# New latency estimates for the planner that orders the attention phases

## The chip, the cores and the metric

The kernel runs on one core of a Trainium2 chip. The metric is the device time of one launch in microseconds (us), the median of several runs. The core's engines are TensorE (PE) for matrix products, VectorE (DVE), ScalarE (ACT), GpSimd (POOL), and SyncE (SP), which issues the DMAs. Each runs its own list of instructions in order, and semaphores make one wait for another.

## The reference

Two consecutive layers of a trunk work on 256 tokens of width 1024, with 256 rows of memory. All is float32.

```python
for layer in range(2):
    x = x + 0.5 * swiglu(rms_norm(x), w_gate, w_up, w_down)
    h = rms_norm(x)
    if layer == 0:   # even: 4 differential heads beside 8 stick-breaking heads, one projection in, one out
        x = x + diff_stickbreak_mixer(h, ...)
    else:            # odd: latent attention, 16 heads, keys and values from a low-rank product, rotary part of 32
        x = x + mla_mixer(h, ...)
    x = x + memory_cross_attention(rms_norm(x), rms_norm(mem), ...)   # 4 heads of 128
    x = x + 0.5 * swiglu(rms_norm(x), w_gate, w_up, w_down)
```

In the latent attention, keys and queries are normalised by head over 96 columns (64 plain and 32 rotated), and the softmax is causal by chunks of 64. In the cross-attention the memory's keys and the queries are normalised by head, and all 256 memory rows are seen.

## The kernel before

The kernel keeps x on the chip and streams all weights. Each float32 product is computed as three matmuls of rounded halves, one each in L284, L285 and L286. So each weight tile that arrives (DMA, L247) is cast by ACT into its high half (L249), and DVE subtracts to get the low half (L251). There are two raw buffers and three slots of halves (`HL`), and a tile is asked for two items ahead of its use (`LOOK`). SP issues the transfers; one that reuses a raw buffer goes out when DVE has read the old tile.

PSUM is cut into banks by purpose: three for products ("mm"), two for scores ("s"), two for turns ("t") and one for attention outputs ("o"). A turn is a transposition by PE (L792), four blocks into one bank, from which ACT or DVE copies them.

The phases are: a feed-forward half, the even mixer (214 to 312 us of the span), the first cross-attention (to about 360), two feed-forward halves, the latent mixer (from about 725), the second cross-attention (to about 890), and a last feed-forward half. PE's order is the program's own. In the attention phases a planner writes it: `run()` (L437) holds several generators (tasks). Each yields what it needs next: banks, a weight, events (`after`), or a pause (`lat`). The planner keeps a clock of its own in which only PE's work costs time (`spend`), and takes the ready task with the lowest priority number. All else is a guess by number: `drop(ps, d)` says that a bank is free d us later, `signal(ev, d)` says that an event is there d us later, and the tables `EST_X0`, `EST_X1`, `EST_AB` and `EST_MLA` hold these d. Arrivals of weights are guessed by `weight_ready` with `WTIME`. These numbers set the order of PE alone, by the order in which the code emits its work; the framework's scheduler then orders ACT, DVE, POOL and SP around it when the program is built.

The names that matter below:

- Even mixer: `values(t)` (L1185) makes the differential heads' output (L1190), whose norm runs over ACT (L1194), DVE (L1196, L1197), POOL (the power, L467) and DVE (L1201). `turn_o` (L1207) turns it, and `out_g` (L653) multiplies it with the output weights in pieces of six matmuls. `mem_k` (L834) makes the memory's keys for the cross-attention; their norm ends in L852, and after `lat` they are turned.
- Cross-attention: `attend(hp)` (L910) for two pairs of heads: scores (L917), softmax (reduction L770, exponentials L779, scaling L784), two turns copied by DVE (L800) and ACT (L798), `out` (L936) and its split into halves (ACT L486, DVE L487). The event `src` releases the output pieces of that pair.
- Latent mixer: `keys(hf, t)` (ACT L1291 to L1294, DVE L1299, L1300, POOL L467, DVE L1313, POOL L1315), `turn_k(hf)` with four turns copied by ACT (L1330), `queries(n, t)` (ACT L1344, L1347; DVE L1352, L1357, L1358, L1362; POOL L1354 and L467), and `attend(n)` (L1427) for four groups of four heads: two turns copied by DVE (L1435), scores (mask L322, L1448), softmax, three turns, `out` (L1481) and its split.

The lines of the functions that the change touches are `yield dict(t=1, lat=7.0)` in `mem_k` and `drop(pt, 0.9)` in `turn_k`.

Of the kernel before, what the change touches and what calls it, by code (L numbers as in the profile page):

```python
# [49 lines left out]
RAW = 2  # L50
BANKS = {"mm": 3, "s": 2, "t": 2, "o": 1}
WTIME = 4.41
SLOTS_MLA = (29, 11)
AB_ORDER = ('ka', 'qa', 'vb', 'va', 'k0', 'k1', 'v0')
T_ORDER = (0, 1)
KRAW = True
PREADD = True

EST_X0 = {'scale': 3.59, 'rq': 1.14, 'psd': 1.46, 'sp': 2.8, 'p1': 4.06, 'p2': 0, 'o': 1.32, 'src': 8.83}
EST_X1 = {'scale': 2.31, 'rq': 1.14, 'psd': 1.46, 'sp': 2.8, 'p1': 3.39, 'p2': 0.0, 'o': 1.18, 'src': 8.83}  # L60
EST_AB = {'b': 1.33, 'va': 1.47, 'rot': 14.92, 'st1': 6.44, 'st2': 0.14, 'z': 1.55, 'sto': 2.4, 'src': 0.79, 'T': 0.74, 'sp': 3.0, 'pc': 8.7, 'pcT': 1.4, 'po': 4.35, 'oa': 8.7, 'srco': 1.25}
PRIO_MLA = [1, 2, 4.2, 3.9, 4.4, 2.3]
PRIO_AB = [1, 6.1, 4.1, 6.9, 6.9, 0.5]
EST_MLA = {'latd': 1.52, 'scale': 11.0, 'r': 1.8, 'kr': 4.06, 'pk': 2.4, 'pv': 1.23, 'v': 1.73, 'k': 6.43, 'kT': 0.9, 'q': 7.82, 'qT': 2.38, 'cs': 3.11, 'sp': 6.25, 'p1': 3.36, 'p2': 0.68, 'p3': 0.75, 'o': 0.58, 'src': 0.8}
MLA_ORDER = (('k', 0), ('kv', 0), ('kv', 1), ('q', 0), ('q', 1), ('k', 1), ('q', 2), ('q', 3), ('v', 0))
HL = 3

# [93 lines left out]
def trunk_kernel(ctx, tc, wflat, xT_d, xtok_d, memT_d, memtok_d, gains_d, rows_d, cst_d, out_d):  # L161
# [34 lines left out]
    def al():  # L196
        return alloc("f")
# [4 lines left out]
    def rel(*ts):  # L202
        for t in ts:
            key, t = ar["own"].pop(id(t))
            ar[key].append(t)

    def sm():
        return T("sm", [P, 16], 24)
# [10 lines left out]
    offs, o = [], 0  # L219
# [92 lines left out]
    def gcol(c):  # L312
        return gains[:, c:c + 1]
# [70 lines left out]
    class Event:  # L384
        t = None
# [8 lines left out]
    def take(tag):  # L394
        ps = ps_(tag)
        i = min(range(len(od.bank[tag])), key=lambda i: od.bank[tag][i])
        od.bank[tag][i] = INF
        od.own[id(ps)] = (tag, i, ps)
        return ps

    def drop(ps, dur):
        tag, i, _ = od.own.pop(id(ps))
        od.pend.append((lambda t, tag=tag, i=i: od.bank[tag].__setitem__(i, t), dur))

    def signal(ev, dur):
        od.pend.append((lambda t, ev=ev: setattr(ev, "t", t), dur))

    def spawn(prio, gen):
        t = Order()
        t.gen, t.prio, t.seq = gen, prio, len(od.all)  # L410
        od.all.append(t)
        t.req = next(gen)
        t.ready = od.now + od.cost + t.req.get("lat", 0.0)
        od.live.append(t)
# [50 lines left out]
    def rsqrt(v, n, dst=None):  # L465
        y = (dst or sm())[:, :n]
        G.tensor_tensor(out=y, in0=v, in1=mhalf[:, 0:n], op=ALU.pow)  # L467
        return y
# [162 lines left out]
    def tm_g(key, xg):  # L631
        yield dict(w=key, mm=1)
        w = weight(key, 256)
        ps = take("mm")
        for t in range(2):
            for k in range(KT):
                a = tuple(z[:, t * P:(t + 1) * P] for z in xg[k])
                mm3(ps[:, t * S:(t + 1) * S], a, (w[0][:, k, :], w[1][:, k, :]), k == 0, k == KT - 1)
                if k % 4 == 3 and (t, k) != (1, KT - 1):
                    yield {}  # L640
        done(key)
        return ps
# [145 lines left out]
    def transpose4(srcs, rows_=P):  # L788

        ps = take("t")  # L790
        for i, s in enumerate(srcs):
            PE.transpose(ps[0:rows_, i * P:(i + 1) * P], s, ident)  # L792
            spend(0.11)
        return ps
# [39 lines left out]
    def mem_k(l, c, events):  # L834

        ps = yield from tm_g((f"memk{l}", c), memstate["x"])
        rm = memstate["rs"]

        def norm():
            yield dict(after=events)  # L840
            k = al()
            for t in range(2):
                A.activation(k[:, t * S:(t + 1) * S], ps[:, t * S:(t + 1) * S], AF.Identity, scale=rm[:, t:t + 1])
            drop(ps, 1.2)
            sq = al()
            G.tensor_tensor(out=sq, in0=k, in1=k, op=ALU.mult)
            v = sm()[:, 0:4]
            V.tensor_reduce(out=v, in_=sq.rearrange("p (a b) -> p a b", b=P), axis=AX.X, op=ALU.add)
            V.tensor_scalar(out=v, in0=v, scalar1=1.0 / P, scalar2=EPS, op0=ALU.mult, op1=ALU.add)
            r = rsqrt(v, 4)  # L850
            k3 = k.rearrange("p (a b) -> p a b", b=P)
            V.tensor_tensor(out=k3, in0=k3, in1=r.unsqueeze(2).to_broadcast([P, 4, P]), op=ALU.mult)  # L852
            yield dict(t=1, lat=7.0)
            pt = transpose4([k3[:, t * 2 + j, :] for j in range(2) for t in range(2)])
            kt = al()
            A.activation(kt, pt, AF.Identity, scale=gcol(G_XK + l))
            drop(pt, 0.9)
            rel(k, sq)
            memstate["k", l, c] = kt

        spawn(1, norm())
# [15 lines left out]
    def cross(l, gc):  # L877
        EST_X = (EST_X0, EST_X1)[l]
        xg = st.xg
# [89 lines left out]
    def mixer_ab(gc):  # L969
# [12 lines left out]
        def products():  # L982
            for key in ("qb", "kb"):
                for c in range(2):
# [5 lines left out]
                    def evac_b(key=key, c=c, ps=ps):  # L990
# [7 lines left out]
                        drop(ps, 0.9)  # L998
                        signal(ev[key, c], EST_AB['b'])

                    spawn(0, after([ev["rb"]], evac_b))
            for key in AB_ORDER:
# [8 lines left out]
                for c in range(2):  # L1011
# [6 lines left out]
                    drop(ps, 1.2)  # L1018
                    signal(ev[key, c], EST_AB['va'])
                if dst is None:  # L1020
# [4 lines left out]
        def rotate(key):  # L1025
# [20 lines left out]
            if key == "qa":  # L1046
                rqs["r"] = r
            signal(ev[key], EST_AB['rot'])


        def strict(z):

            dg = z.rearrange("p (a b) -> p a b", b=S)[:, :, 0:P]
            G.affine_select(out=dg, in_=dg, pattern=[[0, 2], [1, P]], compare_op=ALU.is_gt, fill=0.0,
                            base=0, channel_multiplier=-1)
# [3 lines left out]
        def stick(hq, g):  # L1059
# [25 lines left out]
            for i, (z, (sp, hh, hl)) in enumerate(zip(zs, sps)):  # L1085
                yield dict(lat=EST_AB['st2'] if i else EST_AB['st1'])
                for h_ in (hh, hl):
# [5 lines left out]
                strict(w_)  # L1093
                drop(z, EST_AB['z'])
                ws.append(w_)
                rel(sp, hh, hl)
            yield dict(lat=EST_AB['sto'], o=1 - g, after=[ev["vb", hq]] + [ev["po", hq]] * g)
            if g == 0:
# [126 lines left out]
    def mixer_mla(gc):  # L1225
# [6 lines left out]
        lat = {"ckv": ([], []), "cq": ([], [])}  # L1232
        rl, kk, kf, vt, kT, qf, qv, rqs = {}, {}, {}, {}, {}, {}, {}, {}

        def latent(key, gc0, ps):
# [8 lines left out]
            sqs.append(sq)  # L1244
            drop(ps, EST_MLA['latd'])

        def scale(key, dim):
            yield dict(t=1, lat=EST_MLA['scale'], after=[ev["rs"]])
            sqs = lat[key][1]
            if PREADD:  # L1250
                if len(sqs) == 2:
                    G.tensor_tensor(out=sqs[0], in0=sqs[0], in1=sqs[1], op=ALU.add)
                G.tensor_tensor(out=sqs[0][:, 0:S], in0=sqs[0][:, 0:S], in1=sqs[0][:, S:2 * S], op=ALU.add)
                ps, cs = colsum([[sqs[0][:, t * P:(t + 1) * P]] for t in range(2)], take)
            else:
                ps, cs = colsum([[q[:, j * S + t * P:j * S + (t + 1) * P] for q in sqs for j in range(2)]
                                 for t in range(2)], take)
            rl[key] = latent_scale(cs, 2, dim, st.var)
            rel(*sqs)
            drop(ps, 0.8)  # L1260
            signal(ev["r" + key], EST_MLA['r'])

        def shared_key(krT):

            yield dict(t=1, lat=EST_MLA['kr'], after=[ev["rs"]])
            pt = take("t")
# [17 lines left out]
        def keys(hf, t, pk, pv):  # L1284
# [9 lines left out]
            A.activation(v, pv, AF.Identity, scale=rc[:, t:t + 1])  # L1294
            drop(pk, EST_MLA['pk'])
            drop(pv, EST_MLA['pv'])
            vt[hf].append(v)
# [24 lines left out]
        def turn_k(hf):  # L1322
            kT[hf] = []
            for g in range(4):
                yield dict(t=1, after=[ev["k", hf, t] for t in range(2)])
                a = g // 2
                pt = transpose4([kf[hf][t][a][:, ((2 * g + j) % 4) * 96:((2 * g + j) % 4 + 1) * 96]
                                 for j in range(2) for t in range(2)], 96)
                d = al()
                A.activation(d[0:96, :], pt[0:96, :], AF.Identity, scale=gqk[0:96, :])  # L1330
                kT[hf].append(d)
                drop(pt, 0.9)
                signal(ev["kT", hf, g], EST_MLA["kT"])
                if g % 2:
                    rel(*[kf[hf][t][a] for t in range(2)])
# [185 lines left out]
    with arena(*SLOTS_FFN):  # L1521
        ffn(0, 1, G_FFN + 16, True)
        ffn(1, 0, G_MIX + 8, False, 1)
    with arena(*SLOTS_MLA):
        mixer_mla(G_XM + 8)
# [78 lines left out]
```

## Time and profile before

| what | value |
|---|---|
| median of 3 runs | 1082.94 us (1082.51 to 1085.24) |
| the profiled execution | 1083.22 us |
| its span | 1081.5 us |
| granted TensorE clock | 0.998 of full speed |
| busy: PE / DVE / ACT / POOL | 98% / 72% / 61% / 11% |
| chain that ended last | PE 87%, DVE 5%, ACT 3%, issue 2%, DMA 2%, POOL 1% |
| PE L792 (turn) waits for DVE L852 | 4.1 us, 3 times |
| PE L792 waits for DVE L784 | 2.3 us, once |
| PE L1448 waits for DVE L1435 | 1.6 us, 2 times |
| PE L792 waits for POOL L1315 | 1.6 us, once |
| PE L936 waits for DVE L800 | 1.1 us, 2 times |
| PE L792 waits for ACT L1330 | 0.9 us, once |
| PE L322 waits for ACT L779 | 0.8 us, once |
| PE L1104 waits (issue) | 0.8 us, once |

The busy share tells how much of the span an engine worked; the chain that ended last is followed back from the last instruction, and tells on which engine the time lay. The waits give PE's idle time by the instruction that waited and the one that released it. A row of a timeline gives the start within the span, the duration, the engine, the line, what was written and read, and in brackets the idle time before it with its releaser. A row with x8 is eight instructions one after another.

### The profile page before, as it was taken

What the parts mean: (1) busy time and instruction counts of PE and PEld (TensorE: products, weight loads), DVE (VectorE), ACT (ScalarE), POOL (GpSimd) and SP (SyncE); (2) the same over time, 40 slices, a digit from 0 to 9 for tenths busy, and PEclk for the clock granted to TensorE, in tenths of its full rate; (3) what the DMA queues carried; (4) which work ended last, traced back from release to release, by engine and by line L of the source; (5) the groups of instructions that cost most, each with busy time, mean ns of one, the idle gap of its engine ahead of it and who ended that gap; (6) DMA issues with size and microseconds to landing.
All of it is one profiled execution on the core that took longest, in us unless ns stands there. A gap on an engine that the chain in (4) does not pass through costs nothing.

```text
span 1081.5 us, 23308 instructions
## 1 busy us (share of the span) xinstructions
PE 1059.9 (98%) x9034; PEld 1042.2 (96%) x9034; DVE 782.3 (72%) x1908; ACT 655.3 (61%) x1775; POOL 124.3 (11%) x160
## 2 busy tenths in 40 slices
PE   8999999999899999999999999999889999999998
PEld 8999999998899999999999999999878999999998
DVE  5988766677867877776777777665788778777653
ACT  6767565567755665555666655565866667555542
POOL 0200000134121200000100000002640212000000
PEclk9999999999999999999999999999999999999999
DMA  8776556625245355555556565554241544555561
GB/s 287 247 252 205 207 188 212 195 89 186 84 156 191 120 192 196 195 185 196 204 182 226 197 215 179 186 193 164 99 157 45 163 145 156 196 195 196 185 228 56
DMA packets 51232, 193.36 MB, mean 179 GB/s; under 512 B 5808, under 2 KB 8368, under 8 KB 36016
## 3 DMA queue, kind: packets, MB, share of 16 engines
q1 hardware_dynamic: 50976, 191.81, 52.1%
q8 instruction: 71, 1.16, 0.4%
q14 instruction: 41, 0.34, 0.1%
q10 hardware_dynamic: 144, 0.05, 0.0%
HBM read 190.79 MB, written 1.05 MB: 177 GB/s over the span
## 4 chain that ended last, share of the span: by engine, by line
PE 87%; DVE 5%; ACT 3%; issue 2%; DMA 2%; POOL 1%; SPq 0%; DVEq 0%; ACTq 0%; POOLq 0%
PE mm L284 27%; PE mm L285 27%; PE mm L286 27%; DMA wr<-wflat 2%; DVE wl L251 1%; ACT slotf L779 1%; PE t L792 1%; POOL sm L467 1%; DVE sm L770 1%; PE t L475 0%; PE s L1448 0%; PE s L917 0%; ACT wh L249 0%; POOL sl L467 0%; PE o L1481 0%
## 5 line engine op out<-in xcount | busy, mean ns | idle before, releaser
L249 ACT CAST wh<-wr 128x256 fp32r<-128x256 f32 (+1 forms) x1216 | 440.7, 434 | 289.5 <-PE mm L285 235.2
L251 DVE TENSOR_TENSOR wl<-wr,wh 128x256 fp32r<-128x256 f32 (+1 forms) x1216 | 500.7, 468 | 121.3 <-ACT wh L249 116.6
L284 PE MATMUL mm<-xh,wh 128*128 128x256 f32 x1552 | 429.7, 277 | 1.6 <-ACT wh L270 1.6
L286 PE MATMUL mm<-xh,wl 128*128 128x256 f32 x1552 | 427.8, 276 | 0.0
L285 PE MATMUL mm<-xl,wh 128*128 128x256 f32 x1552 | 427.7, 276 | 0.0
L284 PEld LDWEIGHTS mm<-xh,wh 128*128 128x128 f32 x1552 | 291.4, 188 | 2.4 <-ACT wh L270 2.1
L286 PEld LDWEIGHTS mm<-xh,wl 128*128 128x128 f32 x1552 | 291.4, 188 | 0.6 <-DVE wl L271 0.3
L285 PEld LDWEIGHTS mm<-xl,wh 128*128 128x128 f32 x1552 | 291.4, 188 | 0.4
L284 PE MATMUL mm<-slotr,wh 128*128 128x256 f32 x896 | 247.6, 276 | 0.3 <-ACT slotr L481 0.3
L285 PE MATMUL mm<-slotr,wh 128*128 128x256 f32 x896 | 246.7, 275 | 0.4 <-DVE slotr L482 0.4
L286 PE MATMUL mm<-slotr,wl 128*128 128x256 f32 x896 | 246.6, 275 | 0.0
L284 PEld LDWEIGHTS mm<-slotr,wh 128*128 128x128 f32 x896 | 168.2, 188 | 1.0 <-ACT slotr L481 0.6
L285 PEld LDWEIGHTS mm<-slotr,wh 128*128 128x128 f32 x896 | 168.2, 188 | 0.7 <-DVE slotr L482 0.6
L286 PEld LDWEIGHTS mm<-slotr,wl 128*128 128x128 f32 x896 | 168.2, 188 | 0.0
L530 POOL TENSOR_TENSOR acc<-acc,sq 128x256 f32<-128x256 f32 x49 | 39.2, 801 | 527.4 <-ACT sq L522 526.8
L738 DVE TENSOR_TENSOR slotf<-mm,rb 128x512 f32<-128x512 f32 x43 | 29.7, 691 | 51.6 <-PE mm L286 51.6
L481 ACT ACTIVATE xh<-x,gains 128x256 fp32r<-128x256 f32 x64 | 32.2, 507 | 28.9 <-DVE x L510 26.0
L779 ACT ACTIVATE slotf<-s,sm,sl 128x256 f32<-128x256 f32 (+1 forms) x64 | 32.8, 523 | 20.5 <-DVE sm L773 14.6
L728 DVE TENSOR_TENSOR slotf<-mm,rb 128x512 f32<-128x512 f32 x43 | 29.7, 690 | 20.9 <-PE mm L286 20.6
L510 DVE SCALAR_TENSOR_TENSOR x<-mm,x 128x256 f32<-128x256 f32 x64 | 26.9, 420 | 23.4 <-PE mm L286 23.4
L482 DVE SCALAR_TENSOR_TENSOR xl<-x,gains,xh 128x256 fp32r<-128x256 f32 x64 | 37.0, 582 | 4.2 <-ACT xh L481 4.0
L487 DVE TENSOR_TENSOR slotr<-slotf,slotr 128x512 fp32r<-128x512 f32 (+1 forms) x52 | 35.7, 690 | 3.4 <-ACT slotr L486 3.2
(203 smaller groups left out, 1150.4 us busy)
## 6 DMA issues: line engine op xcount, KB each, us to landing
wr<-wflat SPq DMA_DIRECT2D x118, 1024.0 KB, 4.8
wr<-wflat SPq DMA_DIRECT2D x179, 256.0 KB, 4.0
wr<-wflat SPq DMA_DIRECT2D x16, 768.0 KB, 4.3
slotf<-memT SPq DMA_DIRECT2D x8, 256.0 KB, 3.3
wr<-wflat SPq DMA_DIRECT2D x2, 512.0 KB, 8.0
slotf<-xtok SPq DMA_DIRECT2D x4, 256.0 KB, 7.0
slotf<-memtok SPq DMA_DIRECT2D x4, 256.0 KB, 4.0
out<-x SPq DMA_DIRECT2D x8, 128.0 KB, 2.0
```

The source lines that it names most:

```text
L249: A.copy(hi[:, a:b], raw[:, a:b])
L251: e.tensor_tensor(out=lo[:, a:b], in0=raw[:, a:b], in1=hi[:, a:b].bitcast(F32), op=ALU.subtract)
L284: PE.matmul(out, a[0], b[0], start=first, stop=False, **kw)
L285: PE.matmul(out, a[0], b[1], start=False, stop=False, **kw)
L286: PE.matmul(out, a[1], b[0], start=False, stop=last, **kw)
L481: return (A.activation(hi, src, AF.Identity, scale=g), V.scalar_tensor_tensor(out=lo, in0=src, scalar=g, in1=hi.bitcast(F32), op0=ALU.mult ...
L482: V.scalar_tensor_tensor(out=lo, in0=src, scalar=g, in1=hi.bitcast(F32), op0=ALU.mult, op1=ALU.subtract))
L487: V.tensor_tensor(out=lo, in0=src, in1=hi.bitcast(F32), op=ALU.subtract)
L530: G.tensor_tensor(out=st.acc, in0=st.acc, in1=sq, op=ALU.add)
L728: V.tensor_tensor(out=t.rearrange("p (a b) -> p a b", b=S), in0=pg.rearrange("p (a b) -> p a b", b=S), in1=rbb, op=ALU.mult)
L738: V.tensor_tensor(out=u.rearrange("p (a b) -> p a b", b=S), in0=pu.rearrange("p (a b) -> p a b", b=S), in1=rbb, op=ALU.mult)
L779: A.activation(p[:, i * w:(i + 1) * w], sps[:, i * w:(i + 1) * w], AF.Exp, bias=nb[:, i:i + 1], scale=r, accum_out=sums[:, i:i + 1])
```

## The change

Only numbers change. In both cross phases `o` rises to 1.6 and `src` falls from 8.83 to 2.0. In the even mixer `va`, `sp` and `srco` rise. In the latent mixer `k`, `kT`, `qT` and `p2` rise and `q` falls; one more buffer slot is given to that phase (`SLOTS_MLA`). The memory's keys wait 9.0 instead of 7.0 ahead of their turn, and the bank of a turned key is held 1.6 instead of 0.9 in the planner's account.

```diff
-SLOTS_MLA = (29, 11)
+SLOTS_MLA = (30, 11)
-EST_X0 = {'scale': 3.59, 'rq': 1.14, 'psd': 1.46, 'sp': 2.8, 'p1': 4.06, 'p2': 0, 'o': 1.32, 'src': 8.83}
-EST_X1 = {'scale': 2.31, 'rq': 1.14, 'psd': 1.46, 'sp': 2.8, 'p1': 3.39, 'p2': 0.0, 'o': 1.18, 'src': 8.83}
-EST_AB = {'b': 1.33, 'va': 1.47, 'rot': 14.92, 'st1': 6.44, 'st2': 0.14, 'z': 1.55, 'sto': 2.4, 'src': 0.79, 'T': 0.74, 'sp': 3.0, 'pc': 8.7, 'pcT': 1.4, 'po': 4.35, 'oa': 8.7, 'srco': 1.25}
+EST_X0 = {'scale': 3.59, 'rq': 1.14, 'psd': 1.46, 'sp': 2.8, 'p1': 4.06, 'p2': 0, 'o': 1.6, 'src': 2.0}
+EST_X1 = {'scale': 2.31, 'rq': 1.14, 'psd': 1.46, 'sp': 2.8, 'p1': 3.39, 'p2': 0.0, 'o': 1.6, 'src': 2.0}
+EST_AB = {'b': 1.33, 'va': 2.8, 'rot': 14.92, 'st1': 6.44, 'st2': 0.14, 'z': 1.55, 'sto': 2.4, 'src': 0.79, 'T': 0.74, 'sp': 4.4, 'pc': 8.7, 'pcT': 1.4, 'po': 4.35, 'oa': 8.7, 'srco': 2.2}
-EST_MLA = {'latd': 1.52, 'scale': 11.0, 'r': 1.8, 'kr': 4.06, 'pk': 2.4, 'pv': 1.23, 'v': 1.73, 'k': 6.43, 'kT': 0.9, 'q': 7.82, 'qT': 2.38, 'cs': 3.11, 'sp': 6.25, 'p1': 3.36, 'p2': 0.68, 'p3': 0.75, 'o': 0.58, 'src': 0.8}
+EST_MLA = {'latd': 1.52, 'scale': 11.0, 'r': 1.8, 'kr': 4.06, 'pk': 2.4, 'pv': 1.23, 'v': 1.73, 'k': 8.4, 'kT': 1.5, 'q': 7.0, 'qT': 2.9, 'cs': 3.11, 'sp': 6.25, 'p1': 3.36, 'p2': 1.2, 'p3': 0.75, 'o': 0.58, 'src': 0.8}
-            yield dict(t=1, lat=7.0)
+            yield dict(t=1, lat=9.0)
-                drop(pt, 0.9)
+                drop(pt, 1.6)

```

The instructions and SP's order are the same in both programs. Three places show what the planner makes of the numbers.

ACT in the latent mixer (L1344 and L1347 make a query tile, L1330 copies turned keys, L249 casts a weight). Before:

```order
L1344 ACTIVATE slotf_9740<-mm_10350,sl_10171 128x384
L1330 ACTIVATE slotf_9733<-t_10372,small 96x512
L1347 ACTIVATE slotf_9732<-slotf_9740 128x384
L1330 ACTIVATE slotf_9745<-t_10378,small 96x512
L1344 ACTIVATE slotf_9746<-mm_10384,sl_10171 128x384
L249 CAST wh_10419<-wr_10418 128x512
L1347 ACTIVATE slotf_9750<-slotf_9746 128x384
L1330 ACTIVATE slotf_9751<-t_10406,small 96x512
L1330 ACTIVATE slotf_9737<-t_10412,small 96x512
L249 CAST wh_10419<-wr_10418 128x512 x2
```

After:

```order
L1347 ACTIVATE slotf_9740<-slotf_9739 128x384
L1344 ACTIVATE slotf_9732<-mm_10373,sl_10172 128x384
L249 CAST wh_10408<-wr_10407 128x512
L1347 ACTIVATE slotf_9733<-slotf_9732 128x384
L1330 ACTIVATE slotf_9745<-t_10395,small 96x512
L1330 ACTIVATE slotf_9746<-t_10401,small 96x512
L249 CAST wh_10408<-wr_10407 128x512 x2
L1330 ACTIVATE slotf_9750<-t_10432,small 96x512
L1330 ACTIVATE slotf_9737<-t_10462,small 96x512
```

A cast (the row of L249 without x2) stood behind two L1330; now it stands ahead of them, and all four L1330 come after it.

DVE in the first cross-attention, from the last scaling of the probabilities on (L784; L487 is the low half of a head pair's output, L800 the copy of turned probabilities). Before:

```order
L784 TENSOR_SCALAR slotf_2666<-slotf_2666,sm_4655 128x256 x2
L487 TENSOR_TENSOR slotr_2682<-o_4663,slotr_2682 128x512
L800 COPY slotf_2658<-t_4684 128x512
L251 TENSOR_TENSOR wl_4705<-wr_4703,wh_4704 128x256 x7
L487 TENSOR_TENSOR slotr_2682<-o_4696,slotr_2682 128x512
```

After:

```order
L784 TENSOR_SCALAR slotf_2666<-slotf_2666,sm_4655 128x256 x2
L487 TENSOR_TENSOR slotr_2682<-o_4663,slotr_2682 128x512
L251 TENSOR_TENSOR wl_4686<-wr_4684,wh_4685 128x256 x8
L800 COPY slotf_2658<-t_4711 128x512
L487 TENSOR_TENSOR slotr_2682<-o_4737,slotr_2682 128x512
```

The copy L800 stood right behind the low half of pair 0; now eight weight subtractions stand between them.

ACT at the end of the even mixer (L1194 begins the norm behind the second `values`, L1176 copies turned probabilities, L843 and L871 copy the memory's keys and values, L856 copies its turned keys, L481 makes the high half of the turned output). Before:

```order
L249 CAST wh_3968<-wr_3967 128x512 x4
L1176 COPY slotf_2659<-t_3995 128x512
L856 ACTIVATE slotf_2665<-t_4001,gains 128x512
L1194 ACTIVATE slotf_2662<-o_4019 128x512
L871 ACTIVATE slotf_2672<-mm_3982,small 128x256
L871 ACTIVATE slotf_2679<-mm_3982,small 128x256
L856 ACTIVATE slotf_2669<-t_4061,gains 128x512
L249 CAST wh_4068<-wr_4067 128x512 x4
L481 ACTIVATE slotr_2682<-t_4136,small 128x512
```

After:

```order
L249 CAST wh_3968<-wr_3967 128x512 x4
L856 ACTIVATE slotf_2659<-t_3995,gains 128x512
L871 ACTIVATE slotf_2672<-mm_3982,small 128x256
L871 ACTIVATE slotf_2679<-mm_3982,small 128x256
L1176 COPY slotf_2665<-t_4039 128x512
L249 CAST wh_4046<-wr_4045 128x512 x4
L1194 ACTIVATE slotf_2662<-o_4096 128x512
L856 ACTIVATE slotf_2669<-t_4112,gains 128x512
L481 ACTIVATE slotr_2682<-t_4136,small 128x512
```

Four casts that stood behind L1194 now stand ahead of it, and so do the two L871.

## Rows read from the trace of the kernel before

**Rows 1.** The page's first part: busy us of TensorE and its weight loads
```profile
PE 1059.9 (98%) x9034; PEld 1042.2 (96%) x9034; DVE 782.3 (72%) x1908; ACT 655.3 (61%) x1775; POOL 124.3 (11%) x160
```

**Rows 2.** Busy us (instructions) by stretch: PE, PEld, DVE, ACT, POOL; clock, DMA, GB/s
```profile
790.00:810.00 20.00, 15.97 (x107) 13.67 (x106) 18.53 (x53) 14.05 (x43) 6.35 (x8) 1.00 0.43 142
```

**Rows 3.** Timeline of PE, even mixer: start, us, engine, line, [idle before <-releaser]
```profile
259.97 0.87 PE L1104 MATMUL o<-slotf,slotf 128*64 128x256 f32 x8 [0.79 <-issue]
...
281.26 0.32 PE L322 MATMUL s<-mk,mq 64*128 64x128 f32 x1 [0.79 <-ACT slotf L779]
...
294.98 0.96 PE L792 MATMUL t<-cst,slotf 128*128 128x128 f32 x4 [2.27 <-DVE slotf L852]
```

**Rows 4.** Timeline of ACT and of DVE at the even mixer's end
```profile
300.46 0.60 ACT L1194 ACTIVATE slotf<-o 128x512 f32<-128x512 f32 x1 [3.80 <-PE o L1190]
...
304.48 2.19 ACT L249 CAST wh<-wr 128x512 fp32r<-128x512 f32 x4
...
303.11 0.69 DVE L1201 TENSOR_TENSOR slotf<-o,sm 128x512 f32<-128x512 f32 x1 [1.12 <-POOL sm L467]
```

**Rows 5.** Timelines of PE, ACT and DVE at the first cross-attention's end
```profile
354.03 1.97 PE L936 MATMUL o<-slotf,slotf 128*128 128x256 f32 x8 [0.57 <-DVE slotf L800]
...
355.65 0.47 PE L284 MATMUL mm<-slotr,wh 128*128 128x256 f32 x1
...
358.06 0.28 PE L285 MATMUL mm<-slotr,wh 128*128 128x256 f32 x1
...
356.03 0.59 ACT L486 CAST slotr<-o 128x512 fp32r<-128x512 f32 x1
...
352.60 0.68 DVE L487 TENSOR_TENSOR slotr<-o,slotr 128x512 fp32r<-128x512 f32 x1
...
354.46 2.10 DVE L251 TENSOR_TENSOR wl<-wr,wh 128x256 fp32r<-128x256 f32 x6 [0.24 <-ACT wh L249]
...
356.66 0.69 DVE L487 TENSOR_TENSOR slotr<-o,slotr 128x512 fp32r<-128x512 f32 x1
```

**Rows 6.** Timelines of SP, ACT, DVE, POOL and PE, latent mixer, 775 to 790 us
```profile
779.27 10.26 SPq L247 DMA_DIRECT2D wr<-wflat  x11
...
778.02 0.68 ACT L1330 ACTIVATE slotf<-t,small 96x512 f32<-96x512 f32 x1
...
782.00 0.62 ACT L249 CAST wh<-wr 128x512 fp32r<-128x512 f32 x1 [2.26 <-DMA wr<-wflat]
...
782.96 1.24 ACT L1330 ACTIVATE slotf<-t,small 96x512 f32<-96x512 f32 x2
...
775.28 0.97 DVE L1313 TENSOR_TENSOR slotf<-slotf,sm 128x256 f32<-128x256 f32 x2 [1.75 <-POOL sm L467]
...
776.17 3.07 DVE L251 TENSOR_TENSOR wl<-wr,wh 128x512 fp32r<-128x512 f32 x4
...
783.53 0.29 DVE L1357 TENSOR_TENSOR slotf<-slotf,slotf 128x128 f32<-128x128 f32 x1
...
787.67 1.27 DVE L1435 COPY slotf<-t 96x512 f32<-96x512 f32 x2
...
776.47 3.71 POOL L1354 TENSOR_TENSOR slotf<-slotf,mqb 128x64 f32<-128x64 f32 x6
...
782.68 2.21 POOL L467 TENSOR_TENSOR sl<-sm,small 128x8 f32<-128x8 f32 x1 [2.50 <-DVE sm L1362]
...
784.86 0.69 POOL L1354 TENSOR_TENSOR slotf<-slotf,mqb 128x64 f32<-128x64 f32 x2
...
783.67 1.22 PE L792 MATMUL t<-cst,slotf 128*96 128x128 f32 x8 [0.90 <-ACT slotf L1330]
...
788.40 1.31 PE L1448 MATMUL s<-slotf,slotf 96*128 96x128 f32 x8 [0.59 <-DVE slotf L1435]
```

**Rows 7.** Timeline of PE, latent mixer, scores of the queries 3
```profile
822.82 0.71 PE L1448 MATMUL s<-slotf,slotf 96*128 96x128 f32 x4 [1.01 <-DVE slotf L1435]
```

**Rows 8.** Timeline of PE, second cross-attention, its last `out` product
```profile
884.39 1.97 PE L936 MATMUL o<-slotf,slotf 128*128 128x256 f32 x8 [0.56 <-DVE slotf L800]
```

## The prediction

> **What bounds the kernel now.** I read the page's busy shares first: TensorE (PE) is busy 1059.9 us, 98% of the span [rows 1], so a gain can only come out of its idle time, and a wait that is added in its stream counts in full unless it swallows another. The profiled run took 1083.22 us, 1.72 more than its span and 0.28 more than the median of the runs, 1082.94. Next I read the waits of PE: those with a named releaser that the new numbers aim at lie in the four attention phases, and they are short. Then I cut the span by phase. Between 790 and 810 us, in the latent mixer, PE is busy 15.97 of 20 and VectorE (DVE) 18.53 [rows 2]: there PE is not what sets the time, a chain over DVE, ACT and POOL is. Last I read each engine's own sequence around the waits with the order of the changed program beside it, because every engine runs its list in order: an instruction that waits holds all behind it.
>
> The instructions are the same in both programs, one to one, so nothing is added or removed. What changes is who stands before whom. I follow four places in the order of time.
>
> **1. The even mixer: about −2.0 us.** Three idle times of PE go by the new order: 0.79 at 259.97 (stick-breaking values), 0.79 at 281.26 (a score bank that the exponentials had not left) and 2.27 at 294.98 (the memory keys' turn waiting for their norm, L852) [rows 3]; other matrix products now stand ahead of each. That is −3.85. Given back: the second `values` product (L1190) now stands only one turn (0.6, half of the 1.22 at 783.67 [rows 6]) and three output pieces of six matmuls ahead of `turn_o`. A matmul of this shape takes 0.12 (19 steps between 355.65 and 358.06, 2.41 us [rows 5]), so PE has 0.6 + 18 × 0.12 = 2.8 us to cover its chain: L1194 on ACT, L1196 and L1197 on DVE, the power on POOL, L1201 on DVE. Before, that chain took 3.34 from the start of L1194 at 300.46 to the end of L1201 at 303.80 [rows 4], and 0.38 ahead of it, as from PE's next matmul at 355.65 to L486 at 356.03 [rows 5]: 3.7. So 0.9 is uncovered. Also four weight casts now stand directly in front of L1194 on ACT where they stood behind it; four take 2.19 us [rows 4]. If they have run by then they cost nothing; if they begin when `values` begins, up to 1.6. Their slot is freed by PE, which is earlier too; followed by hand I get 0.95. Sum −3.85 + 0.9 + 0.95 = −2.0. Bounds −3.3 (casts free, half of the rest hidden) and −0.5 (casts in full, and 0.6 for the next wait).
>
> **2. First cross-attention: about +2.0 us.** With `src` at 2.0 the 18 output matmuls of head pair 0 stand ahead of the `out` product of pair 1 (L936); before, they stood behind it. There they were cover: L936's bank is copied by ACT (L486, from 356.03) and subtracted by DVE (L487, to 357.35), and PE needed the subtracted half only at 358.06 [rows 5]. Now the first needer is next in the row. PE leaves L936 at 355.65 and L487 ends 1.7 later; one matmul of 0.1 can go before it. New wait 1.6. The first piece also comes too early at its own end: it stands ahead of the probabilities' turn and needs L487 of pair 0, which ends at 353.28, 0.9 after PE gets there. Gone is the 0.57 in front of L936 [rows 5]. Net +1.9 if L936 itself starts in time. But on DVE eight weight subtractions (L251) now stand ahead of L800, the copy of turned probabilities that L936 needs; before, seven of them stood behind it, six in 2.10 us [rows 5]. They follow L487, so L800 begins not before 353.28 + 8 × 0.35 = 356.1 and L936 at about 356.9, where PE would be there at 356.4. L285 of pair 1 then comes at 356.9 + 1.6 + 1.7 = 360.2 against 358.06, +2.1. I take 2.0; bounds 0.6 (only the uncovered wait less the two gone, half hidden) and 2.4.
>
> **3. Latent mixer: about +5.0 us.** Up to 782 the phase's chain is that of the keys: DVE, POOL's power, DVE; DVE's last L1313 waits 1.75 for POOL, not for PE [rows 6]. So PE's idle time ahead of that is slack, and taking it away gives nothing. Then one place decides.
> a) On ACT a weight cast (L249) waits 2.26 us for its DMA until 782.00. The transfer was issued at 779.27, when DVE had read the last of the raw buffer (four L251 from 776.17) [rows 6]. DVE's order up to there is unchanged, so 782.00 stays. Before, two evacuations of turned keys (L1330) had passed, the second at 778.02; now that cast stands ahead of them, and they end at about 782.00 + 0.5 (cast) + 0.5 (L1347) + 0.62 = 783.6 and 784.2 (two took 1.24 at 782.96 [rows 6]). Both turn banks are held till then.
> b) The turns of the remaining keys and of the first queries go through these two banks one by one, and the last turn of keys needs the bank that DVE's first L1435 empties. Before, from the first L1357 at 783.53 to the end of the first L1435 at 787.67 + 0.64 DVE took 4.8 us, 0.5 of it waiting for POOL's L1354. In the new order POOL's power (2.21 us from 782.68) stands ahead of the rotation L1354 for which that first L1357 waits; before, this rotation was in the run of six at 776.47. With the power ending at 784.5 to 784.9 and one of the two at 0.35, L1357 comes at 785.2, and the first L1435 ends at 785.2 + 4.3 = 789.5 [rows 6].
> c) After it come the turn (0.6, half of the 1.22 at 783.67), 24 matmuls of memory's values at 0.12 = 2.9, and the masked scores, 1.31: 794.3. Before, the scores ended at 788.40 + 1.31 = 789.7 [rows 6]. **+4.6.**
> d) From there DVE has 18.53 us of work in 20 [rows 2], in an unchanged order that begins with the reduction (L770) of that score. So the rest shifts as a block; at most 1.5 can be swallowed.
> e) Behind 810 the wait of 1.01 for the queries 3 goes [rows 7], since their copies stand earlier on DVE. Against it three L251 come ahead of a reduction and of an evacuation (one takes 0.77, four 3.07 [rows 6]), and the last `out` has one output piece as cover instead of more, a new wait of about 0.6 by the chain of step 2. Net +0.4; bounds −1.0 and +1.3.
> Together +5.0; bounds +2.1 (1.5 of d, −1.0 of e) and +6.5.
>
> On POOL and DVE side by side: six L1354 took 3.71 us beside the four L251, 1.24 a pair, and a pair 0.69 at 784.86 [rows 6]. The Trainium skill (SBUF — State Buffer, section "SBUF: two separate sides") says that a DVE operation with two SBUF inputs and a GpSimd operation that reads SBUF share one pair of ports, and that the one which comes second is fully blocked. The rows agree in direction. By that rule the second rotation of step b, which now falls beside L1357 and L251, would take 1.24 rather than 0.69, and the sum would be 6.5 instead of 6.0. I keep 6.0, since L1357 and L251 are issued there one after another with gaps.
>
> **4. Second cross-attention: about +1.0.** The same move, but L800 keeps its place ahead of the weights and the turn its place ahead of the pieces, so the pieces come in time at their own end. New wait 1.6 after L936; gone 0.56 in front of it [rows 8]. Bounds 0.5 and 1.4.
>
> **The sum**: −2.0 + 2.0 + 5.0 + 1.0 = +6.0; 1083.22 + 6.0 = 1089.2 by the profiled run, 1088.9 by the median; I say 1089.0. About 0.3%, 3.25 us, is what a measurement of this kernel can tell from no change.
>
> **Rivals.**
> A. The waits simply go, as the new numbers suppose, and nothing takes their place: 3.85 in the even mixer, 0.57 and 0.56 in the cross phases, 0.90 (783.67), 0.59 (788.40) and 1.01 in the latent mixer [rows 3, 5 to 8]; 7.5 in all, 1075.5. For it: PE is 98% busy, and each of these rows is its idle time. Against it: in three phases the new order puts a needer right behind its maker. 0.12.
> B. Not slower: the transfer of step a lands sooner. Its issue hangs on the four L251. If DVE gets to them 3 us sooner, because the keys' chain was PE's after all, the cast has its data by 779, the two L1330 keep their times and steps a to c fall away: −2.0 + 2.0 + 0.4 + 1.0 = +1.4, 1084.5, no change. It decides from about 3 us. Against it: the 1.75 for POOL at 775.28 [rows 6]. 0.15.
> C. Of the 4.6 the 1.5 us of DVE's idle time between 790 and 810 are swallowed: +4.5, 1087.5. 0.15.
> D. All uncovered waits are larger, casts late in every phase: the upper bounds of three phases, −0.5 + 2.4 + 6.5 + 1.4 = +9.8, 1092.8. 0.08.
> The forecast itself 0.50, from 1086.5 (the latent mixer 2 lower and the even one 0.5) to 1091.5 (the even mixer 1.5 higher, the latent one 1.0).
>
> **Range and chances.** To hold 8 in 10 the range takes in C and B with the forecast, and leaves out A and D: 1083.5 to 1092.0. Faster by over 0.3%: A, 0.12. Within it: B and the forecast's lowest end, 0.18. Slower: 0.70.
>
> **What would show it.** Right: PE waits about 1.6 us for L486 and L487 right after the last L936 of both cross phases; in the latent mixer two L1330 follow a cast that waits for a DMA, PE idles 3 us or more at turns between 783 and 791, and the first L770 of the scores comes 4 to 5 us later after the last L1313; the wait for L852 near 295 is gone and one for L1201 has come ahead of `turn_o`. Wrong: if that cast finds its data there, or if DVE's L1313 stand earlier within the phase, step 3 falls and with it the sign.

## The result and the profile after

The changed kernel takes 1094.07 us (median of 4 runs, 1090.16 to 1094.63) against 1084.09 for the kernel before on the same chip: ratio 1.0091, 95% interval 1.0075 to 1.0106, about 10 us slower. The prediction was 1089.0 with a range up to 1092.0: the sign is right, the size is not. The profiled execution took 1094.63 us, its span is 1092.9, and its mean granted TensorE clock is 0.988 where it was 0.998. The four runs had 0.988, 0.988, 0.990 and 0.995 at 1094.63, 1094.49, 1093.65 and 1090.16 us: the time goes with the clock.

The page's busy line and its row of granted clock in 40 slices:

```profile
PE 1068.3 (98%) x9034; PEld 1048.9 (96%) x9034; DVE 781.9 (72%) x1908; ACT 654.8 (60%) x1775; POOL 123.6 (11%) x160
...
PEclk9999999999989999999999999999889999999999
```

PE is busy 8.4 us longer than in [rows 1], with the same instructions. In three slices the clock is below nine tenths of full speed.

PE's waits (us in total, times, longest):

```profile
PE t L792 <- ACT slotf L1330: 5.1, 1, 5.1
...
PE t L792 <- DVE slotf L784: 3.3, 1, 3.3
...
PE t L792 <- DVE slotf L1201: 2.0, 1, 2.0
...
PE mm L285 <- DVE slotr L487: 1.6, 4, 0.6
...
PE mm L284 <- ACT slotr L486: 1.4, 2, 0.7
...
PE mm L284 <- ACT slotf L871: 1.2, 1, 1.2
```

Most waits of the kernel before are gone or small (L852 has 0.8 left of 4.1); these six have come or grown.

Where the time came, read at the same matmuls of PE's feed-forward lists (us against the profiled run of before): 0.3 ahead of the first mixer, even mixer +0.4, first cross-attention +2.6, latent mixer +7.35, second cross-attention +0.8, in all +11.4.

The rows that answer [rows 3, 4], at the even mixer's end, of ACT, DVE and PE:

```profile
298.59 2.24 ACT L249 CAST wh<-wr 128x512 fp32r<-128x512 f32 x4
...
301.13 0.60 ACT L1194 ACTIVATE slotf<-o 128x512 f32<-128x512 f32 x1 [0.30 <-PE o L1190]
...
300.00 3.10 DVE L251 TENSOR_TENSOR wl<-wr,wh 128x512 fp32r<-128x512 f32 x5
303.01 0.68 DVE L1196 TENSOR_REDUCE sm<-slotf 128x4 f32<-128x512 f32 x1
...
305.01 0.69 DVE L1201 TENSOR_TENSOR slotf<-o,sm 128x512 f32<-128x512 f32 x1 [1.12 <-POOL sm L467]
...
305.76 1.10 PE L792 MATMUL t<-cst,slotf 128*128 128x128 f32 x7 [2.00 <-DVE slotf L1201]
...
307.87 0.58 PE L285 MATMUL mm<-slotr,wh 128*128 128x256 f32 x1 [0.20 <-DVE slotr L482]
...
309.11 0.41 PE L284 MATMUL mm<-slotr,wh 128*128 128x256 f32 x1
```

The wait of 2.27 for the memory keys is gone. Four casts stand ahead of L1194 and are done 0.30 before it starts; behind it five weight subtractions (L251) keep DVE from L1196 until 303.01, 1.3 us after L1194 has ended. L1201 comes at 305.01, and PE waits 2.00 for it. Still the first matmul with the low half of the turned output (L285) starts at 307.87, against 309.72 before. But then one matmul of the same shape lasts 0.41 instead of 0.28, and they follow each other at 0.21 instead of 0.12 us. The stretches say why (columns as in [rows 2]; the third from the end is the granted clock):

```profile
304.00:308.00 4.00, 1.81 (x9) 1.16 (x9) 1.62 (x3) 1.27 (x2) 0.98 (x1) 0.81 1.01 331
...
308.00:312.00 4.00, 4.00 (x19) 4.00 (x20) 0.48 (x1) 0.00 (x0) 0.00 (x0) 0.50 0.15 57
...
785.00:790.00 5.00, 2.95 (x14) 2.89 (x15) 3.68 (x11) 3.80 (x7) 3.19 (x5) 0.50 0.61 176
...
810.00:815.00 5.00, 2.70 (x9) 2.20 (x10) 4.88 (x16) 3.84 (x14) 1.20 (x2) 0.67 0.47 155
...
815.00:820.00 5.00, 5.00 (x30) 3.58 (x29) 3.00 (x8) 2.27 (x8) 0.00 (x0) 0.65 0.55 187
```

From 306.5 to 313.3 us the granted clock is half, the lower of TensorE's two levels; by 313.8 the gain of 1.9 has become a loss. The same happens in the latent mixer from 784.3 to 791.1 and from 811.7 to 818.5. Each fall begins during or right behind a wait of PE.

The rows that answer [rows 5, 8], the two cross phases, of DVE and PE:

```profile
354.35 2.77 DVE L251 TENSOR_TENSOR wl<-wr,wh 128x256 fp32r<-128x256 f32 x8 [0.38 <-ACT wh L249]
...
357.04 0.69 DVE L800 COPY slotf<-t 128x512 f32<-128x512 f32 x1
...
357.78 1.99 PE L936 MATMUL o<-slotf,slotf 128*128 128x256 f32 x8 [0.61 <-DVE slotf L800]
...
360.45 0.38 PE L284 MATMUL mm<-slotr,wh 128*128 128x256 f32 x1 [0.68 <-ACT slotr L486]
...
361.18 0.38 PE L285 MATMUL mm<-slotr,wh 128*128 128x256 f32 x1 [0.34 <-DVE slotr L487]
...
899.72 0.39 PE L285 MATMUL mm<-slotr,wh 128*128 128x256 f32 x1 [0.34 <-DVE slotr L487]
```

Eight weight subtractions stand ahead of L800, L936 starts at 357.78, and the first needer of its split waits 0.68 for the high half and 0.34 for the low one.

The rows that answer [rows 6], latent mixer (3.3 us later throughout, by what came before), of ACT, PE, POOL and DVE:

```profile
785.38 0.62 ACT L249 CAST wh<-wr 128x512 fp32r<-128x512 f32 x1 [5.30 <-DMA wr<-wflat]
...
787.05 1.94 PE L792 MATMUL t<-cst,slotf 128*96 128x128 f32 x8 [5.05 <-ACT slotf L1330]
...
792.51 0.64 PE L792 MATMUL t<-cst,slotf 128*96 128x128 f32 x4 [0.62 <-DVE slotf L1435]
...
787.49 1.20 POOL L1354 TENSOR_TENSOR slotf<-slotf,mqb 128x64 f32<-128x64 f32 x4
...
788.12 0.39 DVE L1357 TENSOR_TENSOR slotf<-slotf,slotf 128x128 f32<-128x128 f32 x1 [1.28 <-POOL slotf L1354]
...
791.78 1.27 DVE L1435 COPY slotf<-t 96x512 f32<-96x512 f32 x2
...
796.99 0.69 DVE L770 TENSOR_REDUCE sm<-s 128x4 f32<-128x512 f32 x1 [3.93 <-PE s L1448]
...
812.30 0.90 PE L792 MATMUL t<-cst,slotf 128*128 128x128 f32 x3 [3.31 <-DVE slotf L784]
...
813.10 2.01 PE L1448 MATMUL s<-slotf,slotf 96*128 96x256 f32 x4
```

The cast waits for its DMA ahead of the turned keys' copies, PE waits 5.05 for these, then 0.62 for L1435; the score's reduction comes at 796.99. Then PE waits 3.31 for scaled probabilities (L784), and the four score matmuls behind it take 2.01 us; four of the same shape at 796.85, at full clock, take 1.08.

### The profile page after: what moved, and what is told of

Same layout as the page of the kernel before. It is cut to its first block, busy times and chain, and to the rows that moved or that the text cites. A ratio compares the mean times of both kernels' runs of the same rounds, so it can differ in the third digit from the quotient of the medians.

```text
span 1092.9 us, 23306 instructions
## 1 busy us (share of the span) xinstructions
PE 1068.3 (98%) x9034; PEld 1048.9 (96%) x9034; DVE 781.9 (72%) x1908; ACT 654.8 (60%) x1775; POOL 123.6 (11%) x160
## 3 DMA queue, kind: packets, MB, share of 16 engines
HBM read 190.79 MB, written 1.05 MB: 176 GB/s over the span
## 4 chain that ended last, share of the span: by engine, by line
PE 65%; DVE 4%; ACT 1%; POOL 1%; issue 1%; DVEq 0%; ACTq 0%
PE mm L285 21%; PE mm L284 20%; PE mm L286 20%; DVE wl L251 2%; POOL sm L467 1%; PE t L792 1%; PE o L936 1%; PE s L1448 1%; ACT slotf L779 1%; PE s L917 1%; PE o L1481 0%; PE t L475 0%; ACT wh L249 0%; DVE sm L770 0%; DVE sm L1358 0%
## 5 line engine op out<-in xcount | busy, mean ns | idle before, releaser
L249 ACT CAST wh<-wr 128x256 fp32r<-128x256 f32 (+1 forms) x1216 | 440.0, 435 | 292.6 <-PE mm L285 235.5
L251 DVE TENSOR_TENSOR wl<-wr,wh 128x256 fp32r<-128x256 f32 (+1 forms) x1216 | 500.0, 468 | 126.5 <-ACT wh L249 122.0
L285 PE MATMUL mm<-xl,wh 128*128 128x256 f32 x1552 | 428.4, 276 | 0.0
L285 PEld LDWEIGHTS mm<-xl,wh 128*128 128x128 f32 x1552 | 292.2, 188 | 0.3
L285 PE MATMUL mm<-slotr,wh 128*128 128x256 f32 x896 | 248.5, 277 | 1.8 <-DVE slotr L487 1.6
L285 PEld LDWEIGHTS mm<-slotr,wh 128*128 128x128 f32 x896 | 169.4, 189 | 2.9 <-DVE slotr L487 2.4
L481 ACT ACTIVATE xh<-x,gains 128x256 fp32r<-128x256 f32 x64 | 32.2, 508 | 29.7 <-DVE x L510 27.4
L792 PE MATMUL t<-cst,slotf 128*128 128x128 f32 (+1 forms) x196 | 29.8, 287 | 12.0 <-ACT slotf L1330 5.1
```

Of the source, the lines that this page charges most:

```text
L249: A.copy(hi[:, a:b], raw[:, a:b])
L251: e.tensor_tensor(out=lo[:, a:b], in0=raw[:, a:b], in1=hi[:, a:b].bitcast(F32), op=ALU.subtract)
L285: PE.matmul(out, a[0], b[1], start=False, stop=False, **kw)
L481: return (A.activation(hi, src, AF.Identity, scale=g), V.scalar_tensor_tensor(out=lo, in0=src, scalar=g, in1=hi.bitcast(F32), op0=ALU.mult ...
```

## Experiments

Theory 1: the order costs what the forecast's steps say, and the granted clock, which falls behind long waits of PE, costs the rest. Theory 2: the chains alone are longer than they were sized. All times are medians beside the kernel before on the same chip. That kernel's median was 1084.09, 1083.08, 1082.29 and 1082.48 on the four occasions, so where two changed kernels of different occasions are compared, the difference of their gaps to before stands beside the difference of the medians.

**pad_waits.** Two of the waits are filled with matmuls of ones into the bank that is then overwritten; the lists of the other engines stay the same.

```diff
-    def transpose4(srcs, rows_=P):
+    def transpose4(srcs, rows_=P, pad=0):
         ps = take("t")
+        [PE.matmul(ps[:, 0:P], ones, ones, start=True, stop=True) for _ in range(pad)]
...
-            pt = transpose4([oa[t][:, (2 * g + j) * P:(2 * g + j + 1) * P] for j in range(2) for t in range(2)])
+            pt = transpose4([oa[t][:, (2 * g + j) * P:(2 * g + j + 1) * P] for j in range(2) for t in range(2)], pad=9 if g == 0 else 0)
...
-                                                               p1[g][:, j * S:j * S + P])])
+                                                               p1[g][:, j * S:j * S + P])], pad=14 if (n, g) == (0, 1) else 0)
```

> The changed kernel with 9 idle matmuls of ones in the bank that turn_o then fills, ahead of its first turn, and 14 in the bank of the first group's second probability turn in the latent mixer; their results are overwritten, no other engine's list changes. They fill two waits of 2.0 and 3.3 us. Theory 1: the granted clock stays at 1.0 behind both, and the kernel gets 4 to 5 us faster, to about 1089.5, near the forecast. Theory 2: the matmuls fill idle time and change nothing, 1094 (within 0.5 us), or they lengthen it.

1089.19 us (before 1083.08; ratio 1.0056, 1.0041 to 1.0071): 4.9 us faster than the changed kernel by the medians and 3.9 by the gaps to before (6.1 against 10.0), with 23 more matmuls. Its stretches, its two rows of idle matmuls (the trace has two records for each), and three rows of DVE in the latent mixer:

```profile
308.00:312.00 4.00, 4.00 (x37) 4.00 (x37) 1.43 (x5) 1.03 (x3) 0.00 (x0) 1.00 0.16 63
...
810.00:815.00 5.00, 4.80 (x38) 3.49 (x37) 4.40 (x16) 2.62 (x11) 0.00 (x0) 1.00 0.60 204
...
815.00:820.00 5.00, 5.00 (x40) 4.96 (x38) 4.88 (x13) 3.65 (x11) 0.61 (x2) 1.00 0.03 11
```

```profile
303.19 2.17 PE L790 MATMUL t<-ones 128*128 128x128 f32 x18
...
805.81 3.29 PE L790 MATMUL t<-ones 128*128 128x128 f32 x28
...
785.25 0.39 DVE L1357 TENSOR_TENSOR slotf<-slotf,slotf 128x128 f32<-128x128 f32 x1 [1.28 <-POOL slotf L1354]
...
788.91 1.27 DVE L1435 COPY slotf<-t 96x512 f32<-96x512 f32 x2
794.10 0.69 DVE L770 TENSOR_REDUCE sm<-s 128x4 f32<-128x512 f32 x1 [3.92 <-PE s L1448]
```

The clock stays at 1.00 in these stretches. By phase against before: even mixer −2.2, first cross-attention +2.6, latent mixer +4.9, second +0.8, together +6.1. Theory 1 holds: the missing term is the granted clock, 2.6 us in the even mixer and 2.4 in the latent one.

**ab_only, x_only, mla_only.** The kernel before with one group of the diff's lines each: `EST_AB` and `lat=9.0`; `EST_X0` and `EST_X1`; `EST_MLA`, `SLOTS_MLA` and `drop(pt, 1.6)`.

> The kernel before with the even mixer's numbers alone (EST_AB, and the memory keys' lat of 9.0). Theory 1 (the order shortens the mixer by 1.9 us up to the first output matmul, then PE's wait of 2 us ahead of turn_o is followed by about 7 us of granted clock 0.5, which gives 2 us back): within 0.3% of before, 0 to +1 us, first output matmul near 307 and one stretch of granted clock 0.5 right behind it. Theory 2 (the forecast's sum, the clock plays no part): -2.0 us. The part of lat in the latent mixer is expected at nothing by both.

> The kernel before with the cross phases' numbers alone (EST_X0, EST_X1). Both theories: +3.0 us by the forecast, +3.4 by the two traces (2.6 and 0.8); granted clock as before, since no wait there is above 0.7 us in one piece. If the sum of the parts is not the whole, one of the three single runs differs from the traces' share by over 1 us.

> The kernel before with the latent mixer's numbers alone (EST_MLA, SLOTS_MLA, the drop of 1.6). Theory 1 (chain of the cast behind a DMA, plus a granted clock of 0.5 after the waits of 5 and 3.3 us): +7 us, two stretches of clock 0.5. Theory 2 (chain alone): +5.0 by the forecast, and no lower clock is needed for it.

Before 1083.08. ab_only 1084.57 (1.0021, 1.0009 to 1.0032), x_only 1087.51 (1.0039, 1.0026 to 1.0052), mla_only 1088.52 (1.0058, 1.0037 to 1.0080): +1.5, +4.4 and +5.4, together 11.4 for the whole change's 10.0. In x_only the cross phases do what both traces say (+2.6 and +0.8 by phase); its median is 1 us above that, and its mean clock, 1.000 in the profiled run, is 0.995 in three of the five. mla_only does not tell the theories apart: its interval, 4.0 to 8.7 us, holds both +5 and +7, and its trace lacks the wait of 3.3 on which theory 1 counted (there is one of 1.77). By phase its latent mixer is +6.35, with two stretches of lower clock. ab_only, above what either theory said, brought the surprise: its even mixer gains 1.4, but the latent mixer loses 3.6, although only `lat` differs there. I had expected nothing of that.

**lat_only.** The memory keys' `lat` alone, in both layers.

```diff
-            yield dict(t=1, lat=7.0)
+            yield dict(t=1, lat=9.0)
```

> The kernel before with the memory keys' lat of 9.0 alone, in both layers. Theory (from ab_only's trace): in the even mixer the 2.3 us in front of the memory keys' turn goes, -2 us; in the latent mixer the turn of the memory keys moves next to the turn of the probabilities, PE's waits of 1.5 and 2.3 us become one of 0.8 and one of 3.3 us, and the granted clock falls to 0.5 behind it, +2 to +3.5 us. Sum 0 to +1.5. Rival (the forecast): -2 us, the latent mixer unchanged.

1082.33 us (1.0000, 0.9991 to 1.0009). By phase −3.9 in the even mixer and +3.65 in the latent one. PE in the latent mixer, and a stretch behind it:

```profile
764.77 1.73 PE L792 MATMUL t<-cst,slotf 128*96 128x128 f32 x7 [3.35 <-POOL slotf L1315]
...
795.96 1.06 PE L792 MATMUL t<-cst,slotf 128*128 128x128 f32 x8 [0.81 <-DVE slotf L852]
...
802.52 0.90 PE L792 MATMUL t<-cst,slotf 128*128 128x128 f32 x3 [3.30 <-DVE slotf L784]
```

```profile
805.00:810.00 5.00, 5.00 (x26) 3.37 (x24) 3.10 (x9) 2.04 (x7) 0.00 (x0) 0.58 0.58 194
```

The kernel before had, at the same turn of the memory keys:

```profile
798.25 0.63 PE L792 MATMUL t<-cst,slotf 128*128 128x128 f32 x4 [1.54 <-DVE slotf L852]
```

Eight L792 in a row: the memory keys' turn now stands right ahead of another turn, so the scores that stood between two waits of 1.54 and 2.29 us do not any more. They have become 0.81 and 3.30, and the clock is 0.58 behind the long one. Of the 3.65, 2.65 come behind that wait. The other 1.0 is there when the first scaled probabilities come, from an earlier place: PE's wait for POOL's L1315 has grown from 1.59 to 3.35, and the granted clock is half from 764.8 to 768.2. Whether the order or the clock makes this 1.0 is not shown.

**after_lat_first_layer.** The changed kernel with the old value in the second layer.

```diff
-            yield dict(t=1, lat=9.0)
+            yield dict(t=1, lat=7.0 if l else 9.0)
```

> The changed kernel with lat 7.0 kept in the second layer. If the joined wait of 3.3 us and the lower clock behind it come from that lat (as lat_only shows against the kernel before): -2.5 to -3.5 us against the changed kernel, about 1091. If they come from EST_MLA: no change, 1094.

1091.38 us (1.0080, 1.0067 to 1.0094): 2.7 us less than the changed kernel by the medians, 1.1 by the gaps to before, whose intervals overlap. So the times do not decide it; the trace does. PE's two waits:

```profile
804.01 0.63 PE L792 MATMUL t<-cst,slotf 128*128 128x128 f32 x4 [1.78 <-DVE slotf L852]
...
810.00 0.66 PE L792 MATMUL t<-cst,slotf 128*128 128x128 f32 x3 [0.90 <-DVE slotf L784]
```

The waits of 0.8 and 3.31 have become 1.78 and 0.90, no stretch of lower clock follows, and the latent mixer is +5.4 by phase where it was +7.35. So 1.9 us come from that `lat`, less than expected. (The even mixer, in the same order, is 0.9 us shorter here, with a shorter stretch of lower clock.)

**casts_on_dve.** pad_waits, with the three casts of the last query tile on DVE; ACT then has no cast ahead of the turned keys' copies.

```diff
-            A.copy(hi[:, a:b], raw[:, a:b])
+            (V.tensor_copy if plan[i][0] == ("uq", 3) else A.copy)(hi[:, a:b], raw[:, a:b])
```

> The kernel of pad_waits with the three casts of one weight tile (the last query tile's) moved from ACT to DVE, so that no cast with a DMA wait stands ahead of the turned keys' copies on ACT; all work is done. Theory A (step a of the forecast, the cast ahead of L1330, holds the score up): PE's wait of 5.0 us goes and the first score's reduction comes about 4 us earlier; 1085.5. Theory B (step b, DVE's late first L1435, holds it alone): PE's wait of 5 us goes, but the reduction comes 1 to 2 us later, by the casts that now stand ahead of that L1435 (0.35 to 0.65 each); 1090 to 1091.

1092.09 us (1.0090, 1.0076 to 1.0104), 2.9 slower than pad_waits by the medians, 3.7 by the gaps to before. PE and DVE, and a stretch:

```profile
785.22 0.40 DVE L1357 TENSOR_TENSOR slotf<-slotf,slotf 128x128 f32<-128x128 f32 x1 [1.28 <-POOL slotf L1354]
...
789.87 1.09 PE L792 MATMUL t<-cst,slotf 128*96 128x128 f32 x4 [4.01 <-DVE slotf L1435]
...
789.14 0.68 DVE L1435 COPY slotf<-t 96x512 f32<-96x512 f32 x1
...
797.04 0.69 DVE L770 TENSOR_REDUCE sm<-s 128x4 f32<-128x512 f32 x1 [6.03 <-PE s L1448]
```

```profile
790.00:795.00 5.00, 5.00 (x24) 4.97 (x25) 1.01 (x2) 0.68 (x1) 0.72 (x1) 0.50 0.60 198
```

The wait of 5.0 for L1330 is gone, and PE waits 4.01 for L1435 instead, which comes at 789.14, 0.2 later than in pad_waits (788.91). The moved casts add about 1 us to DVE's list ahead of it, and one L251 (0.6) now stands behind it, so this time alone does not settle the matter. But the L1357 with which DVE's list starts on the way to L1435 waits 1.28 for POOL in both runs and comes at 785.22 without the cast on ACT and at 785.25 with it. So what holds the last turn of keys is POOL's rotation and DVE's list (step b), not the cast (step a). Of the 2.9 us by which the first reduction (L770) is later, 0.2 are that delay and the rest is again clock: the wait now lies right ahead of the 24 matmuls, and they run at 0.50; in pad_waits the stretch of half clock was over when L1435 came (781.9 to 788.7).

**k_only.** The kernel before with the keys' estimate alone.

```diff
-EST_MLA = {..., 'k': 6.43, ...}
+EST_MLA = {..., 'k': 8.4, ...}
```

> The kernel before with the keys' estimate of 8.4 alone. In the order this number by itself puts the cast with the DMA wait ahead of the turned keys' copies and two turns of keys behind the first queries' turns. If these make the latent mixer's loss: +4 to +5 us of the 5.4 that mla_only lost. If kT, q, qT, p2 or the bank's 1.6 make it: under +1.5.

1086.04 us (1.0032, 1.0021 to 1.0042), +3.75; latent mixer +4.0 in the profiled run, 1.1 of it behind 808 us at a lower clock. This number alone makes most of the latent mixer's loss (2.9 of pad_waits' 4.9, without that clock). The others of `EST_MLA` were not run alone.

**ab_first_layer_pad, lat_first_layer, lat_first_layer_pad.** What is left when only the good part is kept: all even mixer's numbers with `lat` in the first layer and the 9 idle matmuls; `lat` in the first layer alone; the same with 9 idle matmuls in the latent mixer's wait for L784 (the pads as in pad_waits).

```diff
-            yield dict(t=1, lat=7.0)
+            yield dict(t=1, lat=7.0 if l else 9.0)
```

> The kernel before with the even mixer's numbers, lat 9.0 in the first layer only, and the 9 idle matmuls ahead of turn_o; cross phases and latent mixer as before. If the clock theory holds: the even mixer keeps its gain of 2 us (0.6 against those runs of before that have no lower clock), 1081 to 1082.5, faster than both kernels. If not: 1083 or more.

> The kernel before with lat 9.0 in the first layer only. From lat_only's trace: the 2.3 us in front of the memory keys' turn go and nothing comes in their place, the latent mixer stays as before: -2 to -2.5 us, about 1080, faster than both kernels and than ab_first_layer_pad. Rival (the gain of the mixer needs EST_AB too): -1 us or less.

> The same with 9 idle matmuls in front of the probabilities' second turn of the first group in the latent mixer, which fill the wait of 2.3 us there. The clock theory: in the runs where the granted clock falls behind that wait (clock 0.997 or less) it no longer does; 0 to -0.8 us against lat_first_layer, and no run with a lower clock in that stretch. Rival: the wait of 2.3 us never costs clock, 0 or +0.2.

ab_first_layer_pad 1081.86 (0.9989, 0.9980 to 0.9998; before 1082.29). lat_first_layer 1080.29 (0.9978, 0.9969 to 0.9987; before 1082.48). lat_first_layer_pad **1079.41** (0.9971, 0.9959 to 0.9983), the lowest median of all, though its interval overlaps that of lat_first_layer. Its padded wait on PE:

```profile
798.69 2.17 PE L790 MATMUL t<-ones 128*128 128x128 f32 x18
...
801.25 0.66 PE L792 MATMUL t<-cst,slotf 128*128 128x128 f32 x3 [0.28 <-DVE slotf L784]
```

By phase, `lat` alone takes 3.9 from the even mixer, and all its numbers together 2.2: `EST_AB` beside it costs 1.7 (a difference; it was not run alone). In lat_first_layer's profile the latent mixer, whose lists are those of before, is 2.6 us longer than in before's: there the clock fell behind the wait of 2.29, where in before's it did not.

```profile
800.00:805.00 5.00, 3.76 (x14) 3.26 (x15) 4.56 (x17) 2.77 (x11) 1.27 (x2) 0.60 0.40 128
```

With the pad, none of six runs has a mean clock below 0.998 (without it five of eleven have), and the latent mixer takes exactly before's time.

## Why the prediction was wrong in size

**The sum has no term for the granted clock.** "A wait that is added in its stream counts in full" was the premise, and it was too small: a wait of PE can cost itself and then as much again, when the clock falls behind it and PE is the bound there. The size: 2.6 us behind the 2.00 ahead of `turn_o`, 2.4 behind the 3.31 for L784, together 5.0 of the 10 to 11. With both filled, pad_waits is at +6.1, where the sum said +6.0. It could have been seen ahead, since the kernel before has one such stretch behind its 2.27 us of [rows 3]:

```profile
296.00:300.00 4.00, 4.00 (x27) 4.00 (x27) 3.10 (x7) 0.66 (x1) 1.38 (x1) 0.68 0.77 244
```

So 1.6 us of the even mixer's "gain" was that stretch (mla_only and x_only, whose even mixer is that of before, lack it and are 1.6 us shorter there; k_only has it and is not), not the wait. The Trainium skill (TensorE: Matmul & The Clock Gate, section "What's actually happening") says that the clock has two levels, by how busy the array was lately; the traces agree, with 0.21 us from one matmul to the next at 0.50 and 0.12 at 1.00.

**Step 1** (−2.0): with the wait filled, −2.2, but that they agree is luck. The three waits (3.85) went as forecast. With them went 1.6 of lower clock, which the sum did not have. Against them stand the 2.00 ahead of `turn_o` and a wait of 1.2 for L871, which it did not have either: −3.85 − 1.6 + 2.0 + 1.2 = −2.25. The 2.00 was forecast as 0.9 + 0.95, and the 0.95 was wrong in kind: the casts on ACT held nothing up, and DVE's five L251 held L1196 up by 1.3. `lat` alone gives 3.9 (2.3, and 1.6 of clock); `EST_AB` beside it costs 1.7. The step's bounds, by their own terms, are −3.4 and −0.75.

**Step 2** (+2.0): +2.6, past the bound of 2.4. L800 came at 357.04, 356.4 on before's scale, where 356.1 was said: the eight subtractions follow casts, and the first began 0.4 late. The rest of the mechanism stands as written: the gaps of 0.68 and 0.34, counted from one start to the next, are 1.05 and 0.6 beyond a matmul's step, the forecast 1.6 with one matmul between.

**Step 3** (+5.0): +4.9 with the waits filled. a) The times were met (cast at 785.38, 782.1 on before's scale; PE's wait 5.05), but its part in the mechanism was argued, and casts_on_dve shows that it is not on the path. b) decides; the first L1435 ended at 789.1 on that scale, forecast 789.5, and the rotations on POOL took 0.6 a pair (four L1354 in 1.20), not 1.24. c) gave +3.9 (pad_waits' 794.10 less 0.4, against 789.75) for +4.6. d) The rest did shift as a block. e) was +1.0 for +0.4. What the step overlooked is `lat` in the second layer, which joins two waits. At full clock that costs nothing that shows (latent mixer +4.9 with it in pad_waits, +5.4 without it in after_lat_first_layer); with the clock it costs 2.4 (changed kernel) to 2.65 (lat_only). The step's upper bound, +6.5, is 0.6 more than its terms add up to (4.6 + 1.3).

**Step 4** (+1.0): +0.8.

Rival D had the size (+9.8) for another reason, larger chains; pad_waits speaks against it. A, B and C are out: waits went, but others came in their place; the transfer did not land sooner; and the shift of 3.9 at the first reduction was still 4.1 behind it up to 810, so nothing was swallowed.

## What to carry to other kernels

On an engine whose clock depends on its work, list the long waits that a change makes or joins, and ask what stands right behind each; work between two waits can be worth more than the waits themselves. Before a table of estimates is replaced, change one number at a time and one place at a time: here one number in one layer gained 2 us, and the whole change lost 10. And where two chains meet at one instruction, only taking one away tells which of them holds it.

## What the runs showed of the hardware

The granted clock fell to half behind single waits of 2.00, 2.27, 3.3 and 4 to 5 us of PE. It also fell behind one of 1.77 (mla_only, 0.61 from 801 to 805 us) and behind two of 1.0 and 1.1 with one matmul between them (casts_on_dve, 0.52 from 782 to 785 us). Behind waits of one size and one order it fell in some executions and not in others: 2.2 to 2.3 in the even mixer (it fell in before and k_only, not in mla_only and x_only), and 2.29 in the latent one. What tells these apart stays open. Idle matmuls whose results are overwritten kept the clock at 1.00 where they stood, and made the changed kernel 4 to 5 us faster; the 0.9 us of lat_first_layer_pad is not clear of the noise.
